# Eight of the twelve groups of layer 1's conditioning move from layer 0's FFN to the recurrence's projections, in halves of 256 columns

## The chip, the cores and the metric

The kernel runs on one core of one Trainium2 chip. The metric is the device time of one execution in microseconds, as the median of three runs. An execution's profile was taken by the hardware profiler; its time is shown beside the runs.

## What is computed

One inference step of a backbone with two layers over 1152 tokens (128 of a context, 1024 of a latent grid), 1024 features wide. Layer 0 mixes tokens by two kinds of attention, layer 1 by a retention and an RWKV-7 recurrence; each layer ends in a SwiGLU FFN. Before each mixer and each FFN the normalised tokens are shifted and scaled, and the results are gated, by six vectors that come from a conditioning vector. There are two of these, one for the context's tokens and one for the latent's. This is the part that the change concerns:

```python
def ada_modulation(cond, w, b):
    m = (jax.nn.silu(cond) @ w + b)[..., None, :]
    return jnp.split(m, 6, axis=-1)
...
    m_ctx = ada_modulation(c_ctx, w_ada[layer], b_ada[layer])
    m_lat = ada_modulation(c, w_ada[layer], b_ada[layer])
    h_ctx = modulate(rms_norm(ctx, norm_mix_g[layer]), m_ctx[0], m_ctx[1])
    h_lat = modulate(rms_norm(lat, norm_mix_g[layer]), m_lat[0], m_lat[1])
```

`w_ada[layer]` is 1024 x 6144 in float32, 25 MB, and it is needed in full for two vectors. The first two of the six vectors of layer 1 are used at the end of layer 0's FFN, where the tokens of layer 1 are normalised; the third after layer 1's mixer; the last three at and after layer 1's FFN.

## The kernel before

**Stages.** In order of time: normalisation and layer 0's projections and attention (to about 956 us of the span), layer 0's FFN (956 to 1797), the recurrence's projections (`rec_proj`, 1797 to 2360), the recurrence itself (`rec_scan`, 2360 to about 2900), its output (`rec_out`), and layer 1's FFN (from 3049). Nearly everything is a matrix product in a split float32 format: each operand is cast by ScalarE into a high part (`wh`, `hH`) and VectorE or GpSimd takes the rest as the low part (`wl`, `hL`); three matmuls make one product (`mm3`, L80 to L84, and L1724 to L1726).

**Who sets the order.** The program is written as generators that hand control back at `yield`. The main one of a stage calls `next(side)` or `background(rate)` between its steps, at a rate that a counter such as `due` sets, so that side work is mixed in. A scheduler of the tile framework then fixes the order of each engine's instructions ahead of time, from a model of the times; on the chip each engine, and each DMA queue, works off its list in that order and waits where something isn't ready.

**The conditioning.** A group is 512 of the 6144 columns, so a layer has twelve. For layer 0 four groups run early on TensorE; its other eight, and all twelve of layer 1, go through `ada_vec` (L165). For each group it takes the eight row blocks k of 128 rows: SyncE loads a tile `aw` of 128 x 512 (L128), and VectorE multiplies it by the conditioning value of each partition, once for each of the two vectors, into the accumulator `aacc` (L179 for the first block, L181 for the others). After the eighth block TensorE sums over the partitions with a column of ones (L189: eight small matmuls in the code, sixteen in the trace), and VectorE adds the bias (`ada_mod`, L149, L153). The load of a block is issued right after the instructions on the block before it. A group is nine steps (`yield`s).

**Where layer 1's twelve groups ran.** All in layer 0's FFN. `ffn` (L1615) first makes the two first tiles of 128 hidden columns plainly, then the others (f = 2 to 21) as seven products of blocks each (L1724 to L1726, operands `hH`, `T1`, `T2`, `T3`; results `A`, `B`, `D`, `E` in PSUM). From the fifteenth product on it calls `next(side)` at a rate of 0.44 (L1755). Then `ffn_out` (L1844) does the output projection in six groups of hidden tiles and calls it at 0.48 (L1898). In the first part `self.ap` is the FFN's own pool (L2079), which gives the tag `aw` no number of buffers, and so one; in the second part `aw` is another name for `raw` (L1802), of which layer 0 has five and layer 1 six (L2074). `raw` holds the FFN's weights before the split.

**The recurrence's projections.** `rec_proj` goes through 15 blocks of 256 columns of `w_in_rec` (`proj_cols`, L788 on). For a block, eight weight tiles `wraw` of 128 x 256 are loaded by SyncE (L793, four buffers), cast to `wh` by ScalarE (L74) and their low part made by VectorE (L75); `wh` and `wl` have nine buffers each, so one tile of the next block fits beside the eight of the present one. Then come 9 tiles of tokens (L817 to L819) or 6 tiles of features (L82 to L84), in four PSUM banks `mm`. Each tile ends in a `sink`: ScalarE copies it into `fst` (two buffers) and SyncE stores it (L834, L844). `background(rate)` is called twice per tile: it advances the preparation of the RWKV operands (`prep`, on ScalarE, VectorE and GpSimd) and the retention (`ret`).

## Time and profile before

| | us |
|---|---|
| median of three runs | 3854.85 |
| lowest and highest run | 3852.91, 3861.53 |
| the profiled execution | 3851.15 |
| its span | 3849.4 |

Times inside the profile count from the start of the span. A row of a view by stage gives the stretch, its length, and for each engine the busy time and, as x, the number of instructions, then the granted TensorE clock as a share of full speed, the share of time in which the DMA engines were busy, and GB/s. Engines are PE (TensorE), PEld (its weight loads), DVE (VectorE), ACT (ScalarE), POOL (GpSimd) and SPq (SyncE's instruction queue, which issues DMAs). A row of a group or a timeline names line, engine, operation, result <- operands, shape and number; what stands in brackets or behind a bar is the idle time ahead of it and what ended it. A waiting row reads: who <- for whom: us in total, times, the longest.

### The profile page before, as it was taken

What the parts mean: (1) busy time and instruction counts of PE and PEld (TensorE: products, weight loads), DVE (VectorE), ACT (ScalarE), POOL (GpSimd) and SP (SyncE); (2) the same over time, 40 slices, a digit from 0 to 9 for tenths busy, and PEclk for the clock granted to TensorE, in tenths of its full rate; (3) what the DMA queues carried; (4) which work ended last, traced back from release to release, by engine and by line L of the source; (5) the groups of instructions that cost most, each with busy time, mean ns of one, the idle gap of its engine ahead of it and who ended that gap; (6) DMA issues with size and microseconds to landing.
All of it is one profiled execution on the core that took longest, in us unless ns stands there. A gap on an engine that the chain in (4) does not pass through costs nothing.

```text
span 3849.4 us, 67037 instructions
## 1 busy us (share of the span) xinstructions
PE 3661.5 (95%) x24885; PEld 3444.4 (89%) x24885; DVE 2272.7 (59%) x5106; ACT 1404.6 (36%) x3361; POOL 1100.4 (29%) x1450
## 2 busy tenths in 40 slices
PE   7999997999999999999999998999998999999998
PEld 4899996999899999999989886877777899999998
DVE  6677864665945556665244556766665774444434
ACT  3445444555333333225332333233322533334221
POOL 2000002112222224333011323665662322324430
PEclk9999997999999999999999998999999999999999
DMA  6433325542223334442334336232223212223321
GB/s 209 125 94 107 113 69 133 133 109 61 64 85 108 91 99 143 149 137 86 106 105 130 115 129 212 58 88 65 65 60 108 62 60 75 75 73 107 116 88 61
DMA packets 425399, 392.16 MB, mean 102 GB/s; under 512 B 68172, under 2 KB 370376, under 8 KB 423536
## 3 DMA queue, kind: packets, MB, share of 16 engines
q1 hardware_dynamic: 406640, 376.29, 32.3%
q10 hardware_dynamic: 13152, 7.27, 0.7%
q0 software_dynamic: 5280, 4.31, 0.6%
q8 instruction: 197, 3.23, 0.3%
q14 instruction: 130, 1.06, 0.1%
HBM read 289.32 MB, written 98.33 MB: 101 GB/s over the span
## 4 chain that ended last, share of the span: by engine, by line
PE 74%; DVE 8%; DMA 8%; POOL 3%; issue 2%; ACT 2%; SPq 0%; DVEq 0%; ACTq 0%; POOLq 0%
PE mm L82 8%; PE mm L84 8%; PE mm L83 8%; PE A L1726 3%; PE A L1724 3%; PE A L1725 3%; PE o L482 3%; DMA aw<-in_w_ada_dram 2%; PE E L1724 2%; PE E L1725 2%; PE mm L350 2%; PE E L1726 2%; PE mm L352 2%; PE mm L351 2%; DVE aacc L181 2%
## 5 line engine op out<-in xcount | busy, mean ns | idle before, releaser
L729 DVE SCALAR_TENSOR_TENSOR x<-mm,mod,x 128x128 f32<-128x128 f32 (+1 forms) x576 | 277.2, 512 | 238.7 <-PE mm L84 237.9
L1636 POOL TENSOR_TENSOR wl<-raw,wh 128x512 fp32r<-128x512 f32 x120 | 167.1, 1392 | 567.2 <-ACT wh L1635 541.3
L1635 ACT CAST wh<-raw 128x512 fp32r<-128x512 f32 x288 | 178.3, 620 | 306.4 <-PE A L1725 107.4
L181 DVE SCALAR_TENSOR_TENSOR aacc<-aw,v,aacc 128x512 f32<-128x512 f32 x280 | 228.7, 849 | 75.2 <-DMA aw<-in_w_ada_dram 74.7
L350 PE MATMUL mm<-wh,hH 128*128 128x384 f32 x576 | 200.8, 349 | 11.5 <-ACT wh L74 4.7
L352 PE MATMUL mm<-wh,hL 128*128 128x384 f32 x576 | 195.8, 341 | 4.6 <-DVE hL L261 4.6
L351 PE MATMUL mm<-wl,hH 128*128 128x384 f32 x576 | 197.3, 342 | 1.0 <-DVE wl L75 0.9
L82 PE MATMUL mm<-hH,wh 128*128 128x384 f32 x528 | 184.6, 351 | 2.6 <-ACT wh L74 2.6
L84 PE MATMUL mm<-hH,wl 128*128 128x384 f32 x528 | 180.3, 344 | 3.4 <-DVE rst L867 2.1
L83 PE MATMUL mm<-hL,wh 128*128 128x384 f32 x528 | 180.3, 342 | 0.0
L1636 DVE TENSOR_TENSOR wl<-raw,wh 128x512 fp32r<-128x512 f32 x168 | 118.8, 708 | 102.1 <-ACT wh L1635 98.3
L397 POOL TENSOR_TENSOR rm<-rm,rm 128x128 f32<-128x128 f32 (+1 forms) x40 | 27.0, 676 | 461.2 <-DVE rm L387 329.0
L75 DVE TENSOR_TENSOR wl<-wraw,wh 128x256 fp32r<-128x256 f32 (+1 forms) x184 | 90.1, 508 | 108.3 <-ACT wh L74 78.7
L1150 PE MATMUL A<-AR,BK 64*128 64x256 f32 x576 | 116.8, 418 | 31.3 <-DVE KK L1154 18.6
L524 ACT ACTIVATE P<-S,mx 128x384 f32<-128x384 f32 (+1 forms) x200 | 112.2, 570 | 88.8 <-DVE mx L522 86.6
L82 PE MATMUL mm<-mh,owh 128*128 128x384 f32 x384 | 138.5, 375 | 5.2 <-ACT owh L74 2.7
L83 PE MATMUL mm<-ml,owh 128*128 128x384 f32 x384 | 132.5, 345 | 0.0
L84 PE MATMUL mm<-mh,owl 128*128 128x384 f32 x384 | 131.3, 342 | 1.2 <-DVE owl L75 1.2
L350 PEld LDWEIGHTS mm<-wh,hH 128*128 128x128 f32 x576 | 110.2, 191 | 16.2 <-ACT ist L368 7.7
L817 PE MATMUL mm<-wh,hH 128*128 128x256 f32 x432 | 124.0, 290 | 0.0
L1150 PEld LDWEIGHTS A<-AR,BK 64*128 64x128 f32 x576 | 75.4, 194 | 53.1 <-issue 20.0
L818 PE MATMUL mm<-wl,hH 128*128 128x256 f32 x432 | 122.4, 285 | 0.0
(540 smaller groups left out, 12501.5 us busy)
## 6 DMA issues: line engine op xcount, KB each, us to landing
raw<-in_w_ffn_in_dram SPq DMA_DIRECT2D x176, 256.0 KB
aw<-in_w_ada_dram SPq DMA_DIRECT2D x160, 256.0 KB
raw<-hdr SPq DMA_DIRECT2D x132, 192.0 KB
hdr<-c SPq DMA_DIRECT2D x160, 144.0 KB
raw<-in_w_ffn_out_dram SPq DMA_DIRECT2D x88, 256.0 KB
F<-stg SPq DMA_DIRECT2D x34, 640.0 KB
stg<-st SPq DMA_DIRECT2D x12, 1536.0 KB
qkv<-ist SPq DMA_DIRECT2D x72, 192.0 KB
```

Of the source, the lines that this page charges most:

```text
L82: mm(out, lhsT=wh, rhs=xh, start=first, stop=False)
L83: mm(out, lhsT=wh, rhs=xl, start=False, stop=False)
L84: mm(out, lhsT=wl, rhs=xh, start=False, stop=last)
L181: nc.vector.scalar_tensor_tensor(acc[:, c, :], w[:, 0, :], s, acc[:, c, :], op0=ALU.mult, op1=ALU.add)
L350: mm(pt[:, :ncol], lhsT=hH[k][:, c], rhs=WH[k], start=k == 0, stop=False)
L351: mm(pt[:, :ncol], lhsT=hH[k][:, c], rhs=WL[k], start=False, stop=False)
L352: mm(pt[:, :ncol], lhsT=hL[k][:, c], rhs=WH[k], start=False, stop=k == KT - 1)
L729: self.nc.vector.scalar_tensor_tensor(x[f][:, c], pt[:, a:b], self.mod[l][jg][:, f, cd : cd + 1], x[f][:, c], op0=ALU.mult, op1=ALU.add)
L1636: eng.tensor_tensor(wl, w, wh, op=ALU.subtract)
L1724: mm(o, lhsT=wh[:, ks], rhs=xh, start=new and k == 0, stop=False, skip_group_check=True)
L1725: mm(o, lhsT=wh[:, ks], rhs=xl, start=False, stop=False, skip_group_check=True)
L1726: mm(o, lhsT=wl[:, ks], rhs=xh, start=False, stop=k == 3, skip_group_check=True)
```

## The change

Layer 0's FFN keeps groups 0 to 3 of layer 1, in its output projection alone, where they still use the buffers of `raw`; the calls in the products go, and with them the FFN's own `aw` and `aacc` buffers in that part. `raw` gets six buffers in both layers. Groups 4 to 11 go to `rec_proj`: `background` calls their generator at a rate of 0.72 for each of the 216 times it is called, whatever else it does. `ada_vec` gets the pool and a width: with 256 it goes through a group in two halves, each with its own eight loads (128 x 256, 128 KB), its own accumulation, four of L189's eight matmuls and its own additions. The pool of `rec_proj` names no number of buffers for `aw`, so there is one, and one of `aacc`. The matmuls' results take one of the four PSUM banks `mm`.

The core of the diff:

```diff
-    def ada_load(self, l, cg, k, n, pool):
-        w = self.t(pool, [P, n, 512], tag="aw")
+    def ada_load(self, l, cg, k, n, pool, c0=0, w=512):
+        t = self.t(pool, [P, n, w], tag="aw")
...
-        self.nc.sync.dma_start(w, src[:, k : k + n, cg * 512 : (cg + 1) * 512])
-        return w
+        self.nc.sync.dma_start(t, src[:, k : k + n, cg * 512 + c0 : cg * 512 + c0 + w])
+        return t
...
-    def ada_vec(self, l, cgs):
+    def ada_vec(self, l, cgs, pool, wd=512):
...
-        w, acc, p2 = self.ada_load(l, cgs[0], 0, 1, self.ap), None, None
-        for n, cg in enumerate(cgs):
+        seq = [(cg, c0) for cg in cgs for c0 in range(0, 512, wd)]
+        w, acc, p2 = self.ada_load(l, cgs[0], 0, 1, pool, 0, wd), None, None
+        for n, (cg, c0) in enumerate(seq):
             for k in range(KT):
                 if k == 0:
                     if p2 is not None:
-                        self.ada_mod(l, cgs[n - 1], p2)
-                    acc = self.t(self.ap, [P, 2, 512], tag="aacc", bufs=1)
+                        self.ada_mod(l, *was, wd)
+                    acc = self.t(pool, [P, 2, wd], tag="aacc", bufs=1)
...
             p2 = self.t(self.nps, [P, 512], tag="mm")
-            for f in range(4):
+            was = cg, p2, c0
+            for f in range(wd // P):
...
+            side, owed = self.ada_vec(1, range(4, 12), p, 256), 0.0
...
             def background(rate):
 
-                nonlocal due
+                nonlocal due, owed
+                owed += 0.72
+                while owed >= 1:
+                    owed -= 1
+                    next(side, None)
...
             while preps:
                 background(1.0)
+            fin(side)
...
-        C, store, due = {}, [], 0.0
-        self.nps = _Alias(ps.pool, {"mm": "D"})
+        C, store = {}, []
...
-            if n >= 14:
-                due += 0.44
-                while due >= 1:
-                    due -= 1
-                    next(side, None)
...
-        self.nps, self.ap = ps, _Alias(p, {"aw": "raw"})
...
-            p = _Bufs(es.enter_context(self.pool(f"ff{l}", "right" if l else "left")), {"raw": 6 if l else 5, "wh": 3, "wl": 3, "c": 4})
+            p = _Bufs(es.enter_context(self.pool(f"ff{l}", "right" if l else "left")), {"raw": 6, "wh": 3, "wl": 3, "c": 4})
...
-            side = iter(()) if l else self.ada_vec(1, range(12))
+            side = iter(()) if l else self.ada_vec(1, range(4), _Alias(p, {"aw": "raw"}))
```

How the order of the instructions changes, at the places of which the prediction speaks. Line numbers in the new order are those of the changed file, one to nine higher than before; x2 is one instruction for each of the two vectors.

VectorE in the middle of layer 0's products, at about 1217 to 1229 us of the profile before (`c` and `raw` are the FFN's tiles, `wl` its weight splits):

```order
L1798 TENSOR_TENSOR c_13651<-c_13583,c_13651 128x288
L1772 TENSOR_TENSOR c_13774<-c_13774,B_13794 128x288
L181 SCALAR_TENSOR_TENSOR aacc_13789<-aw_13938,v_5_67,aacc_13789 128x512 x2
L1772 TENSOR_TENSOR c_13775<-c_13775,B_13807 128x288
L1636 TENSOR_TENSOR wl_13825<-raw_13662,wh_13824 128x512
L181 SCALAR_TENSOR_TENSOR aacc_13789<-aw_14055,v_5_67,aacc_13789 128x512 x2
L181 SCALAR_TENSOR_TENSOR aacc_13789<-aw_14125,v_5_67,aacc_13789 128x512 x2
L1636 TENSOR_TENSOR wl_13891<-raw_13660,wh_13890 128x512
L1786 TENSOR_TENSOR c_13920<-c_13918,E_13864 128x288
```

and at a like place after the change:

```order
L1801 TENSOR_TENSOR c_13823<-c_13759,c_13823 128x288
L1799 TENSOR_TENSOR c_13760<-c_13760,E_13780 128x288
L1645 TENSOR_TENSOR wl_13908<-raw_13699,wh_13907 128x512
L1801 TENSOR_TENSOR c_13824<-c_13760,c_13824 128x288
L1775 TENSOR_TENSOR c_13938<-c_13938,B_13952 128x288
L1775 TENSOR_TENSOR c_13939<-c_13939,B_13965 128x288
L1645 TENSOR_TENSOR wl_13983<-raw_13835,wh_13982 128x512
L1707 TENSOR_TENSOR raw_14086<-raw_13950,raw_14086 128x512
L1645 TENSOR_TENSOR wl_14045<-raw_13833,wh_14044 128x512
L1789 TENSOR_TENSOR c_14074<-c_14072,E_14018 128x288
```

The instructions on `aacc` are gone from the products; the rest stands as before.

VectorE in the projections where the run of splits of the fourth block begins (the last splits of the third block ahead of it, at about 1880 us; `kd` belongs to the retention), before:

```order
L75 TENSOR_TENSOR wl_20532<-wraw_20529,wh_20531 128x256
L75 TENSOR_TENSOR wl_20538<-wraw_20535,wh_20537 128x256
L75 TENSOR_TENSOR wl_20796<-wraw_20793,wh_20795 128x256
L1454 TENSOR_SCALAR kd_21236<-rk_21084,KD_20031 128x9x64 x2
L75 TENSOR_TENSOR wl_20802<-wraw_20799,wh_20801 128x256
L75 TENSOR_TENSOR wl_20808<-wraw_20805,wh_20807 128x256
L75 TENSOR_TENSOR wl_20814<-wraw_20811,wh_20813 128x256
L75 TENSOR_TENSOR wl_20820<-wraw_20817,wh_20819 128x256
```

and after the change:

```order
L182 SCALAR_TENSOR_TENSOR aacc_20439<-aw_20442,v_5_67,aacc_20439 128x256 x2
L182 SCALAR_TENSOR_TENSOR aacc_20439<-aw_20474,v_5_67,aacc_20439 128x256 x2
L182 SCALAR_TENSOR_TENSOR aacc_20439<-aw_20493,v_5_67,aacc_20439 128x256 x2
L75 TENSOR_TENSOR wl_20604<-wraw_20601,wh_20603 128x256
L182 SCALAR_TENSOR_TENSOR aacc_20439<-aw_20525,v_5_67,aacc_20439 128x256 x2
L75 TENSOR_TENSOR wl_20610<-wraw_20607,wh_20609 128x256
L75 TENSOR_TENSOR wl_20616<-wraw_20613,wh_20615 128x256
L75 TENSOR_TENSOR wl_20622<-wraw_20619,wh_20621 128x256
L75 TENSOR_TENSOR wl_20628<-wraw_20625,wh_20627 128x256
L182 SCALAR_TENSOR_TENSOR aacc_20439<-aw_20542,v_5_67,aacc_20439 128x256 x2
L75 TENSOR_TENSOR wl_20634<-wraw_20631,wh_20633 128x256
```

Pairs of instructions on `aacc`, each with a load of its own, now stand ahead of the run and inside it.

SyncE at the same place: the stores of the third block's results (`rvd`) and the loads of weights (`wraw`), before:

```order
L834 DMA rvd<-fst_20734 128x256
L834 DMA rvd<-fst_20762 128x256
L793 DMA wraw_20823<-in_w_in_rec_dram 128x256
L793 DMA wraw_20829<-in_w_in_rec_dram 128x256
L793 DMA wraw_20835<-in_w_in_rec_dram 128x256
L793 DMA wraw_21009<-in_w_in_rec_dram 128x256
L834 DMA rvd<-fst_20790 128x256
L793 DMA wraw_21015<-in_w_in_rec_dram 128x256
```

and after the change:

```order
L837 DMA rvd<-fst_20488 128x256
L128 DMA aw_20493<-in_w_ada_dram 128x256
L837 DMA rvd<-fst_20520 128x256
L128 DMA aw_20525<-in_w_ada_dram 128x256
L837 DMA rvd<-fst_20556 128x256
L796 DMA wraw_20625<-in_w_in_rec_dram 128x256
L128 DMA aw_20542<-in_w_ada_dram 128x256
L796 DMA wraw_20631<-in_w_in_rec_dram 128x256
L796 DMA wraw_20637<-in_w_in_rec_dram 128x256
L837 DMA rvd<-fst_20588 128x256
```

Loads of `aw` now stand between the stores and among the loads of weights. Over the stage there are 128 of them, in the first 14 of the 15 blocks; between one run of splits and the next stand 8 to 11.

## The prediction

> **What bounds the kernel now.** The page comes first: its span and TensorE's share.

> ```profile
> span 3849.4 us, 67037 instructions
> PE 3661.5 (95%) x24885; PEld 3444.4 (89%) x24885; DVE 2272.7 (59%) x5106; ACT 1404.6 (36%) x3361; POOL 1100.4 (29%) x1450
> ```

> TensorE is busy for 95% of the span, so a microsecond is won only where TensorE waits, or where it does work that could go. The profiled execution took 3851.15 us, of which 1.75 us lie around the span; the median of the runs is 3854.85, 3.7 us above it. I work against the execution and add the 3.7 at the end.

> Next the busy time by stage. Both layers run the same FFN code, but only layer 0's carries the conditioning, so the two FFNs are a controlled pair. The rows are, in order: layer 0's FFN before its products of blocks (L1724 to L1726), their first three column tiles, the other seventeen, and the output projection; then the recurrence's projections; then the four FFN stretches again for layer 1.

> ```profile
> core 0: us, PE busy (x) PEld busy (x) DVE busy (x) ACT busy (x) POOL busy (x), PEclk, DMA share, GB/s
> 956.20:1016.40 60.20, 56.37 (x303) 54.60 (x303) 55.20 (x113) 25.83 (x52) 17.37 (x11) 0.94 0.26 76
> 1016.40:1094.00 77.60, 71.32 (x505) 70.24 (x506) 54.70 (x106) 29.31 (x65) 23.36 (x17) 0.96 0.23 68
> 1094.00:1505.60 411.60, 396.49 (x2953) 394.17 (x2953) 232.36 (x397) 139.61 (x298) 119.63 (x92) 0.99 0.34 100
> 1505.60:1795.10 289.50, 289.50 (x1712) 289.12 (x1710) 189.40 (x345) 78.17 (x155) 110.65 (x101) 1.00 0.42 133
> 1797.00:2360.00 563.00, 548.84 (x3745) 494.75 (x3747) 269.30 (x758) 183.06 (x428) 107.19 (x106) 0.99 0.38 121
> 3048.90:3103.10 54.20, 53.95 (x303) 53.59 (x304) 46.58 (x110) 28.73 (x61) 12.53 (x13) 0.97 0.18 55
> 3103.10:3176.30 73.20, 70.47 (x507) 69.45 (x506) 46.39 (x94) 27.86 (x61) 26.14 (x17) 0.95 0.23 70
> 3176.30:3554.90 378.60, 378.60 (x2857) 378.60 (x2857) 166.22 (x305) 144.77 (x300) 118.98 (x92) 1.00 0.27 80
> ```

> The same two stretches of layer 0, for the conditioning's own matmuls (L189) alone:

> ```profile
> 1094.00:1505.60 411.60, 11.03 (x96) 11.28 (x96) 0.99 0.34 100
> 1505.60:1795.10 289.50, 11.03 (x96) 11.55 (x96) 1.00 0.42 133
> ```

> 2953 matmuls less these 96 are 2857, exactly layer 1's number, yet layer 0 takes 411.6 us against 378.6. The waits of TensorE and then of VectorE in that stretch say why:

> ```profile
> PE A L1726 <- DVE wl L1636: 10.4, 5, 2.3
> PE E L1724 <- DVE c L1786: 4.6, 3, 1.8
> ```

> ```profile
> DVE aacc L181 <- DMA aw<-in_w_ada_dram: 51.7, 29, 2.9
> ```

> One such case in order of time, on SyncE's queue, VectorE and TensorE:

> ```profile
> 1223.80 0.33 SPq L128 DMA_DIRECT2D aw<-in_w_ada_dram  x1
> 1228.02 0.33 SPq L128 DMA_DIRECT2D aw<-in_w_ada_dram  x1
> ```

> ```profile
> 1226.58 1.41 DVE L181 SCALAR_TENSOR_TENSOR aacc<-aw,v,aacc 128x512 f32<-128x512 f32 x2 [2.81 <-DMA aw<-in_w_ada_dram]
> 1227.91 0.68 DVE L1636 TENSOR_TENSOR wl<-raw,wh 128x512 fp32r<-128x512 f32 x1
> ...
> 1230.79 2.26 DVE L181 SCALAR_TENSOR_TENSOR aacc<-aw,v,aacc 128x512 f32<-128x512 f32 x2 [1.83 <-DMA aw<-in_w_ada_dram]
> ...
> 1233.58 0.68 DVE L1636 TENSOR_TENSOR wl<-raw,wh 128x512 fp32r<-128x512 f32 x1
> ```

> ```profile
> 1234.31 0.61 PE L1726 MATMUL A<-hH,wl 128*128 128x288 f32 x1 [2.29 <-DVE wl L1636]
> ```

> The pool has one buffer for `aw`. VectorE waits for the load (1223.80 to 1226.58: 2.78 us), uses it in two instructions (1.41), and only then the next load goes out at 1228.02: a round of 4.2 us. The weight splits `wl` stand behind such pairs, and TensorE in the end behind a split: the one of 1233.58 held it for 2.29 us.

> **The change part by part.**

> *Layer 0's FFN, products.* All `aacc` rows (the accumulator's) have left the products, as the order in the section on the change shows at the place quoted above; the four groups that stay come in the output projection. What is left is layer 1's program, in which TensorE waits for nothing (378.6 busy of 378.6), so I see nothing that would be late next, and the seventeen tiles should take layer 1's time: 378.6 - 411.6 = **-33.0** (15.1 of it idle TensorE, 11.0 its L189, 6.9 matmuls drawn out after stalls). The 60.2 + 77.6 us ahead of them are 10.4 above layer 1's 54.2 + 73.2. VectorE does a first group there, by the row of the `aacc` instructions alone,

> ```profile
> 956.00:1016.40 60.40, 0.00 (x0) 0.00 (x0) 13.22 (x16) 0.94 0.26 77
> ```

> and `raw` has five buffers against layer 1's six; the change cures both, but part of the rest may be layer 0's own start. Between 0 and -10.4 I take **-6**.

> *Output projection.* Six groups' L189 took 11.03 us there; four remain: two groups at 1.84 are **-3.7**. TensorE has no idle time in this stretch, so nothing else is to be had.

> *Recurrence's projections, TensorE.* The eight groups' matmuls are as many in halves as whole: 128 of the recorded instructions at 11.03/96 = 0.115, **+14.7**. TensorE is busy 548.8 of 563 us here, so all of it counts.

> *The same, VectorE, loads and stalls.* For the times:

> ```profile
> L181 DVE SCALAR_TENSOR_TENSOR aacc<-aw,v,aacc x280: 726/745/1850, 38.5 to 1713.0; 128x512 f32<-128x512 f32 x140
> ```

> ```profile
> L729 DVE SCALAR_TENSOR_TENSOR x<-mm,mod,x 128x256 f32<-128x256 f32 x144 | 68.3, 474 | 0.0
> ```

> ```profile
> 1904.61 0.81 SPq L793 DMA_DIRECT2D wraw<-in_w_in_rec_dram  x2
> ```

> ```profile
> 1906.70 0.41 ACT L74 CAST wh<-wraw 128x256 fp32r<-128x256 f32 x1 [1.07 <-DMA wraw<-in_w_in_rec_dram]
> ```

> ```profile
> DVE mod L149 <- PE mm L189: 4.1, 4, 1.1
> ```

> A half instruction costs 0.474, not half of 0.745: 256 of them are about 115 us (a few are the cheaper first ones). They fit by volume: 269 of 563 us become 384. A load of 128 KB, the new size, took 2.09 us to its first use (1904.61 to 1906.70). There is again one buffer, so a round is 2.1 + 0.9 + 0.1 to wake SyncE = 3.1 us, and each of 16 halves adds about 1.0 for the turn of the accumulator. 128 rounds are 413 us in the 505 that the weight loads span:

> ```profile
> L793 SPq DMA_DIRECT2D wraw<-in_w_in_rec_dram x150: 327/382/1634, 1797.0 to 2302.3; - x150
> ```

> The rows above give the price of halving: the round falls from 4.2 to 3.1, not to 2.1. [...]

> On average the rounds fit; locally they don't. The runs of weight splits mark the blocks of 256 columns (VectorE, then TensorE's use of the sixth split of the middle run):

> ```profile
> 1854.48 1.50 DVE L75 TENSOR_TENSOR wl<-wraw,wh 128x256 fp32r<-128x256 f32 x4 [12.50 <-ACT wh L74]
> 1880.12 1.49 DVE L75 TENSOR_TENSOR wl<-wraw,wh 128x256 fp32r<-128x256 f32 x4 [12.39 <-ACT wh L74]
> 1883.10 0.43 DVE L75 TENSOR_TENSOR wl<-wraw,wh 128x256 fp32r<-128x256 f32 x1 [1.49 <-ACT wh L74]
> 1904.15 1.94 DVE L75 TENSOR_TENSOR wl<-wraw,wh 128x256 fp32r<-128x256 f32 x4 [18.91 <-PE mm L83]
> ```

> ```profile
> 1883.20 0.51 PE L84 MATMUL mm<-hH,wl 128*128 128x384 f32 x2
> 1884.96 0.34 PE L84 MATMUL mm<-hH,wl 128*128 128x384 f32 x1
> ```

> Around 1880.12, VectorE did nothing but splits, and SyncE's queue held only result stores and weight loads. In the new order, shown in the section on the change, pairs of `aacc` instructions stand inside the run of splits, and `aw` loads between the stores and the weight loads. An `aw` load waits for VectorE to free the buffer, and the stores and weight loads behind it wait too. The order holds 11 rounds between the runs of 1854.48 and 1880.12, 25.6 us plus 0.9 of new matmuls: 11 x 3.1 + 1.0 = 35.1, late by 8.6. The next 24.0 + 0.9 us hold nine, 28.9: late by 4.0. Of these 12.6 us about 4 are in hand (the second split, done by 1880.5, is used at 1883.20, the sixth, done at 1883.53, at 1884.96): 8. In the other blocks the rounds fit: 108 x 3.1 + 14 = 349 us in the 505.3 - 49.6 = 455.7 that are left. What stalls there is the run of splits: by the order 17 pairs stand inside runs, each holding the rest back by up to 2.6 us against 1.4 to 2.7 in hand; half a microsecond each on average makes 9. So **+17**. The lower end is 5: 12.6 less the 2.7 and less the 4.8 from 1880.12 to 1884.96. The upper is 36: 17 pairs at 2.1, the mean of the five waits on `wl` above (10.4/5), nearest in kind but with less in hand. A gain is excluded, since nothing is taken away in this stage.

> Its end stays as it is: the last pair stands ahead of the last block's splits, whose loads end at 2302.3, and the stage ends at 2360. Costed at nothing: 128 issues on SyncE at 0.33 (42 us of its 563), 16.8 MB more (121 becomes 151 GB/s, against 133 in the output projection today, where TensorE does not wait), and a PSUM bank of the four that the projections turn through, held for one step of the chain. If that cover fails, the case is B below.

> Sum: -33.0 - 6 - 3.7 + 14.7 + 17 = **-11.0** us: 3851.15 becomes 3840.2, and the median of runs 3843.9.

> **The rivals.** *A, the stalls hide:* 5 instead of 17, net -23.0, 3832. For it: VectorE is idle over half the stage. Against: 51.7 us of waits for only 43 loads in the FFN, by the row

> ```profile
> aw<-in_w_ada_dram SPq DMA_DIRECT2D x43, 256.0 KB
> ```

> *B, the chain of loads becomes the bound,* the slower side. Rounds fill the 505.3 us plus the 42.7 gained from (505.3 + 42.7 - 16)/128 = 4.16 us on. Large transfers pass on the same queue:

> ```profile
> stg<-st SPq DMA_DIRECT2D x12, 1536.0 KB
> ```

> At 4.4 us a round the chain is 579, 74 over, in place of 14.7 + 17: +31 net, 3886. For it: the FFN's measured 4.2. Against: that is with double loads and instructions. [...]

> *C, the boundaries eat the gain:* 28 of stalls, net 0, 3855. For it: SyncE held up at the very time when the last three weights of a block are asked for. That the change does not relieve the FFN is not a rival: no `aacc` row is left in the products.

> **How the numbers follow.** About 0.2%, 7.7 us, is what a measurement can tell from no change. Forecast 0.43 (stalls 10 to 24, net -18 to -4), A 0.19, C 0.22 (-4 to +8), B 0.16. Faster: A and three quarters of the forecast, 0.51. Same: the other quarter and 0.18 of C, 0.29. Slower: 0.20. Range: lowest -33 - 10 - 3.7 + 14.7 + 5 = -27; highest -33 + 0 - 3.7 + 14.7 + 36 = +14; with 1 us on each side 3827 to 3870. It leaves out most of B.

> **What would show it.** Layer 0's products at 379 us for seventeen tiles, with no wait for `aw`; L189 in the projections at about 15 us; the rounds at 3.1; TensorE's waits for `wl` at the block boundaries. I am wrong if the projections grow by over 45 us, or if layer 0's seventeen tiles stay above 390.

## The result, and the profile after

The changed kernel takes 3920.8 us (median of four runs, 3918.1 to 3928.5) against 3855.2 before on the same chip: a ratio of 1.0171, 95% interval 1.0151 to 1.019. It is slower by 66 us, where 11 us faster were forecast, and outside the range. Its profiled execution, the slowest of the four, took 3928.5 us; the rows below are of it, so they have to explain 77 us against the profile before, some 12 more than the medians differ by. The page of the changed kernel:

```profile
span 3926.7 us, 67300 instructions
PE 3709.8 (94%) x24885; PEld 3487.6 (89%) x24885; DVE 2273.1 (58%) x5244; ACT 1408.3 (36%) x3361; POOL 1096.2 (28%) x1450
PEclk9999998999999999998999996988888999999999
```

and the row of the clock in 40 slices before:

```profile
PEclk9999997999999999999999998999999999999999
```

TensorE does the same 24885 recorded instructions and is busy 48 us longer. In slices 25 and 27 to 31, where the recurrence runs, the granted clock has fallen. The stages are cut at four marks that both kernels have: the first matmul on `T3h` in layer 0's FFN, the first use of a weight's low part in the projections, the same in their last block, and the first matmul on `T3h` in layer 1's FFN. A row gives the stretch, its length, and per engine busy time and instructions; the last three numbers are clock, DMA share and GB/s. Before:

```profile
956.20:1801.00 844.80, 814.96 (x5471) 808.63 (x5471) 537.43 (x976) 276.18 (x576) 272.60 (x219) 0.98 0.36 108
1801.00:2306.20 505.20, 504.03 (x3391) 454.68 (x3392) 232.70 (x657) 167.14 (x390) 88.65 (x82) 1.00 0.37 116
2306.20:3048.90 742.70, 675.37 (x5078) 569.08 (x5077) 483.03 (x1115) 231.56 (x540) 382.09 (x799) 0.94 0.30 90
3048.90:3849.40 800.50, 785.68 (x5319) 783.90 (x5319) 385.12 (x758) 269.20 (x566) 244.92 (x199) 0.99 0.27 82
```

and after:

```profile
960.00:1760.70 800.70, 789.35 (x5344) 786.62 (x5344) 435.50 (x838) 280.34 (x576) 267.69 (x219) 0.99 0.30 93
1760.70:2325.90 565.20, 527.20 (x3482) 476.76 (x3483) 337.78 (x926) 162.16 (x383) 87.33 (x80) 0.97 0.42 130
2325.90:3126.60 800.70, 729.37 (x5116) 615.30 (x5114) 479.86 (x1122) 237.41 (x547) 385.08 (x801) 0.88 0.29 86
3126.60:3926.70 800.10, 783.93 (x5319) 782.27 (x5319) 386.28 (x758) 268.33 (x566) 243.75 (x199) 0.99 0.27 82
```

So layer 0's FFN gained 44.1 us; the projections lost 60.0; the third stretch (the end of the projections, the recurrence and its output, "the scan" from here on) lost 58.0; 3.8 us are lost ahead of the FFN, where nothing was changed, and 0.4 gained behind: 3.8 - 44.1 + 60.0 + 58.0 - 0.4 = 77.3, the difference of the two spans. The recurrence got no new instruction; of the moved work only the last 8 of the 128 small matmuls, about 1 us, lie in the third stretch.

The same rows show what kind of time was lost. In the scan TensorE's busy time rose from 675.37 to 729.37 us, by 54.0, for the same work, and its idle time (length less busy) only from 67.3 to 71.3. In the projections it is the other way: idle time rose from 1.2 to 38.0 us, busy time by 23.2, most of which is the moved matmuls.

**The FFN.** The seventeen tiles of the products after the change:

```profile
1088.60:1467.40 378.80, 378.80 (x2859) 378.80 (x2858) 167.34 (x305) 144.00 (x298) 118.73 (x91) 1.00 0.26 80
```

They take layer 1's 378.6 us to within 0.2, as forecast, and TensorE has no idle time.

**The projections.** What VectorE's instructions on `aw` waited for there (times in us, number of times, the longest), and the matmuls that read the sums:

```profile
DVE aacc L182 <- DMA aw<-in_w_ada_dram: 137.3, 83, 4.8
DVE mod L149 <- PE mm L192: 25.6, 9, 7.8
```

```profile
L192 PE MATMUL mm<-ones,aacc 128*128 128x1 f32 x120 | 16.6, 248 | 18.2 <-DVE aacc L182 18.2
```

TensorE stood 18.2 us ahead of these matmuls. One such end of a half, first on VectorE, then on TensorE:

```profile
1818.67 0.87 DVE L182 SCALAR_TENSOR_TENSOR aacc<-aw,v,aacc 128x256 f32<-128x256 f32 x2
1821.79 0.88 DVE L182 SCALAR_TENSOR_TENSOR aacc<-aw,v,aacc 128x256 f32<-128x256 f32 x2 [2.25 <-DMA aw<-in_w_ada_dram]
1824.98 0.88 DVE L182 SCALAR_TENSOR_TENSOR aacc<-aw,v,aacc 128x256 f32<-128x256 f32 x2 [2.30 <-DMA aw<-in_w_ada_dram]
1828.07 0.88 DVE L182 SCALAR_TENSOR_TENSOR aacc<-aw,v,aacc 128x256 f32<-128x256 f32 x2 [2.21 <-DMA aw<-in_w_ada_dram]
1831.21 0.88 DVE L182 SCALAR_TENSOR_TENSOR aacc<-aw,v,aacc 128x256 f32<-128x256 f32 x2 [2.26 <-DMA aw<-in_w_ada_dram]
```

```profile
1831.84 0.56 PE L192 MATMUL mm<-ones,aacc 128*128 128x1 f32 x2 [7.78 <-DVE aacc L182]
```

Five rounds stand one behind the other in VectorE's list, with nothing between them. Each takes 3.1 us, the forecast length, of which VectorE stands 2.2; everything that is queued behind, and TensorE in the end, waits. Of TensorE's 38 us of idle time in this stage about 35 were ended by VectorE. For weights that came late it hardly waited, neither for the high parts (first row) nor for the splits (the other two), so it was not the weight loads behind the `aw` loads in SyncE's queue that held it:

```profile
PE mm L82 <- ACT wh L74: 0.2, 1, 0.2
PE mm L84 <- DVE wl L75: 2.7, 3, 1.3
PE mm L821 <- DVE wl L75: 1.4, 1, 1.4
```

By the records of the clock TensorE was granted half its clock for 10.2 us from 1826.4, that is 2.3 us after the wait of 7.78 us began, and again for 13.7 us from 1857.2, inside the wait at the next such end. Over the projections it ran 35 us at half clock, before 3.

**The scan.** The same records give 85 us at half clock before and 195 after: half of the difference, 55 us, is about the 54.0 by which TensorE's busy time grew. Its idle time is hardly larger: the wait that holds it longest there, for VectorE's copies `KK`, is 17.1 us between 2400 and 2920 us before, and 18.8 in the same length from 2420 us after. But it waits otherwise. Before and after:

```profile
PE A L1150 <- DVE KK L1154: 17.1, 15, 1.5
```

```profile
PE A L1159 <- DVE KK L1163: 18.8, 9, 3.6
```

Fewer waits, and longer ones. One of these places on TensorE, before:

```profile
2540.93 1.14 PE L1150 MATMUL A<-AR,BK 64*128 64x256 f32 x8
2542.50 0.66 PE L1224 MATMUL I<-ident,MM 128*128 128x128 f32 x4 [0.43 <-DVE MM L1244]
2542.99 1.06 PE L1235 MATMUL I<-E,TC 128*128 128x128 f32 x8
2545.51 2.15 PE L1150 MATMUL A<-AR,BK 64*128 64x256 f32 x8 [1.46 <-DVE KK L1154]
```

and after:

```profile
2707.76 1.16 PE L1159 MATMUL A<-AR,BK 64*128 64x256 f32 x8
2708.84 1.16 PE L1249 MATMUL I<-X,WT 128*128 128x128 f32 x8
2713.43 1.82 PE L1159 MATMUL A<-AR,BK 64*128 64x256 f32 x5 [3.42 <-DVE KK L1163]
```

The matmuls `A` of a step come in four sets, and matmuls `I` of another step stand between the sets. Ahead of the last set the trace has 12 of them before and 8 after, and 3.42 us of idle time in one piece instead of 0.43 and 1.46. The copies `KK` come late because VectorE's own list has the copy `BT` ahead of them, and that waits for GpSimd, 0.72 us before and 2.05 after the change:

```profile
2543.16 1.33 DVE L1203 COPY BT<-MB 32x256 f32<-32x256 f32 x1 [0.72 <-POOL MB L1201]
```

```profile
2711.28 1.33 DVE L1212 COPY BT<-MB 32x256 f32<-32x256 f32 x1 [2.05 <-POOL MB L1210]
```

The clock follows at once, in stretches of 3.41 us after the change:

```profile
2707.04:2710.45 3.41, 2.96 (x24) 1.00 0.14 53
2710.45:2713.87 3.42, 0.44 (x2) 1.00 0.00 0
2713.87:2717.28 3.41, 3.41 (x12) 0.50 0.13 19
2717.28:2720.69 3.41, 3.41 (x19) 0.50 0.12 19
2720.69:2724.11 3.42, 3.42 (x22) 0.50 0.10 10
```

The order in which the scheduler put TensorE's instructions at this place of a step, before and after:

```
L1150 MATMUL A_27889<-AR_5513_27745,BK_5514_27750 128x256 x2
L1150 MATMUL A_27890<-AR_5513_27745,BK_5514_27750 128x256 x2
L1224 MATMUL I_27654<-ident_60,MM_27310 128x128 x4
L1235 MATMUL I_27660<-E_27518,TC_4986_25679 128x128 x4
L1150 MATMUL A_27901<-AR_5522_27770,BK_5523_27775 128x256 x2
```

```
L1159 MATMUL A_28171<-AR_5593_28027,BK_5594_28032 128x256 x2
L1159 MATMUL A_28172<-AR_5593_28027,BK_5594_28032 128x256 x2
L1249 MATMUL I_27949<-X_27947,WT_27935 128x128 x4
L1159 MATMUL A_28183<-AR_5602_28052,BK_5603_28057 128x256 x2
```

The program text of the scan was not touched, and its instructions are the same; the scheduler's model arrived at another order of them, by up to 66 places on TensorE. It repeats from step to step.

### The profile page after: what moved, and what is told of

Read it like the earlier page. It is cut to its first block, busy times and chain, and to the rows that moved or that the text cites. A ratio compares the mean times of both kernels' runs of the same rounds, so it can differ in the third digit from the quotient of the medians.

```text
span 3926.7 us, 67300 instructions
## 1 busy us (share of the span) xinstructions
PE 3709.8 (94%) x24885; PEld 3487.6 (89%) x24885; DVE 2273.1 (58%) x5244; ACT 1408.3 (36%) x3361; POOL 1096.2 (28%) x1450
## 3 DMA queue, kind: packets, MB, share of 16 engines
q14 instruction: 131, 1.07, 0.1%
## 4 chain that ended last, share of the span: by engine, by line
PE 67%; DMA 12%; DVE 10%; POOL 3%; issue 3%; ACT 2%; SPq 0%; DVEq 0%; ACTq 0%; POOLq 0%
PE mm L82 7%; PE mm L84 6%; PE mm L83 6%; DMA aw<-in_w_ada_dram 4%; PE A L1733 3%; PE A L1734 3%; PE A L1735 3%; PE o L485 3%; DVE aacc L182 3%; PE E L1734 2%; PE E L1733 2%; PE E L1735 2%; PE mm L353 2%; PE mm L355 2%; PE mm L354 2%
## 5 line engine op out<-in xcount | busy, mean ns | idle before, releaser
L182 DVE SCALAR_TENSOR_TENSOR aacc<-aw,v,aacc 128x256 f32<-128x256 f32 (+1 forms) x392 | 242.6, 656 | 146.5 <-DMA aw<-in_w_ada_dram 145.9
L84 PE MATMUL mm<-hH,wl 128*128 128x384 f32 x528 | 181.1, 346 | 5.0 <-DVE wl L75 2.7
L83 PE MATMUL mm<-hL,wh 128*128 128x384 f32 x528 | 181.3, 344 | 0.0
L1159 PE MATMUL A<-AR,BK 64*128 64x256 f32 x576 | 133.4, 448 | 31.8 <-DVE KK L1163 19.7
L1707 DVE TENSOR_TENSOR raw<-raw,raw 128x512 f32<-128x512 f32 x40 | 27.7, 692 | 193.9 <-POOL raw L1706 193.9
L1159 PEld LDWEIGHTS A<-AR,BK 64*128 64x128 f32 x576 | 85.5, 209 | 55.8 <-issue 24.4
L83 PE MATMUL mm<-ml,owh 128*128 128x384 f32 x384 | 133.8, 348 | 0.0
L84 PE MATMUL mm<-mh,owl 128*128 128x384 f32 x384 | 131.8, 343 | 0.9 <-DVE owl L75 0.9
## 6 DMA issues: line engine op xcount, KB each, us to landing
raw<-in_w_ffn_in_dram SPq DMA_DIRECT2D x176, 256.0 KB
aw<-in_w_ada_dram SPq DMA_DIRECT2D x96, 256.0 KB
raw<-in_w_ffn_out_dram SPq DMA_DIRECT2D x88, 256.0 KB
stg<-st SPq DMA_DIRECT2D x12, 1536.0 KB
```

The lines of the kernel that those rows point to most:

```text
L83: mm(out, lhsT=wh, rhs=xl, start=False, stop=False)
L84: mm(out, lhsT=wl, rhs=xh, start=False, stop=last)
L182: nc.vector.scalar_tensor_tensor(acc[:, c, :], w[:, 0, :], s, acc[:, c, :], op0=ALU.mult, op1=ALU.add)
L1159: mm(pts[h][:, j * 256 : j * 256 + 256], lhsT=BK[hs, j, :], rhs=AR[hs], start=True, stop=True)
```

## The experiments

Two things had to be explained: the 58 us of the scan (order, or something that the moved work leaves behind), and the growth of the projections beyond 31.7 us. The table has what the twelve kernels gave; lengths and the us at half clock are of one profiled execution each, between the marks used above, and the waits are VectorE's idle time in the projections until an `aw` load. The profiled executions of e4, e6, e7, e10 and e11 took 13, 17, 10, 4 and 16 us less than their kernel's median, so their lengths lie rather low.

| kernel | median us | ratio to before, 95% | projections | half clock there | waits for `aw` | scan | half clock there |
|---|---|---|---|---|---|---|---|
| before | 3855.2 | | 505.2 | 3 | 0 | 742.7 | 85 |
| after | 3920.8 | 1.0151 to 1.019 | 565.2 | 35 | 141 | 800.7 | 195 |
| e1 | 3870.5 | 1.0032 to 1.0073 | 572.2 | 55 | 144 | 741.3 | 75 |
| e2 | 3893.5 | 1.009 to 1.0123 | 505.0 | 3 | 0 | 779.6 | 157 |
| e3 | 3803.4 | 0.9858 to 0.9891 | 508.3 | 7 | 0 | 739.6 | 89 |
| e4 | 3910.4 | 1.012 to 1.0194 | 593.8 | 68 | 116 | 743.2 | 58 |
| e5 | 3872.7 | 1.0049 to 1.0099 | 574.9 | 41 | 163 | 738.7 | 79 |
| e6 | 3837.7 | 0.9952 to 0.9993 | 532.8 | 14 | 47 | 732.4 | 51 |
| e7 | 3838.5 | 0.995 to 0.9981 | 534.0 | 21 | 43 | 734.9 | 55 |
| e8 | 3864.5 | 1.0026 to 1.0065 | 553.3 | 24 | 105 | 749.3 | 106 |
| e9 | 3828.9 | 0.9932 to 0.9968 | 534.7 | 23 | 0 | 736.4 | 65 |
| e10 | 3831.3 | 0.9944 to 0.9987 | 531.0 | 14 | 18 | 734.0 | 75 |
| e11 | 3849.3 | 0.9961 to 1.0009 | 532.2 | 12 | 46 | 738.2 | 75 |
| e12 | 3875.5 | 1.0055 to 1.0087 | 569.3 | 42 | 141 | 744.7 | 82 |

The kernel before took 3849.7, 3851.8 and 3849.0 us beside the three sets of four (e1 to e4, e5 to e8, e9 to e12), each of which ran on a chip of its own.

**e1 and e2: the scan's order exchanged.** The edit notes the instructions that `rec_scan` traces and chains those of each engine in a given order (`SCAN_ORDER`, read from the other kernel's schedule); the chain says only which comes first (`NoSync`).

```diff
+    def pin(self, i0):
+        dep = lambda: mybir.DependencyInfo(mybir.DependencyClass.NoSync, mybir.DependencyReason.DATA)
+        ins = [i for i in list(self.nc.cur_bb.bb.instructions)[i0:] if type(i).__name__ != "BassTilePoolBoundary"]
+        for e, moves in json.loads(zlib.decompress(base64.b85decode(SCAN_ORDER))).items():
+            own = [i for i in ins if str(i.engine) == "EngineType." + e]
+            own = [own[n + m] for n, m in enumerate(moves)]
+            for a, b in zip(own, own[1:]):
+                self.tc.add_manual_dep(b, a.name, dep(), reason="pin")
...
+            i0 = len(self.nc.cur_bb.bb.instructions)
             self.rec_scan(hp)
+            self.pin(i0)
```

> The changed kernel, with the instructions of rec_scan held on every engine in the order that they had before. Theory 1 (the order): the scan lost its time because its instructions were put in another order, which gathers TensorE's idle time and lowers the granted clock; then about 3866 us (3855 to 3880), with 85 to 110 us of the scan at half clock instead of 195. Rival (what the moved work leaves behind: buffers, transfers, a later start): 3921 us, give or take 5, half clock as in the changed kernel.

> The kernel before, with the instructions of rec_scan held in the order that they have in the changed kernel, and nothing else. Theory 1 (the order): slower by the 55 us that the scan lost, 3895 to 3915 us, with about 170 to 200 us of the scan at half clock. Rival (what the moved work leaves behind): 3855 us, as before.

Both came out by the order. The changed kernel with the old order in the scan (e1; its projections and its scan):

```profile
1752.60:2324.80 572.20, 536.44 (x3483) 485.27 (x3484) 338.30 (x927) 162.68 (x384) 88.61 (x81) 0.95 0.41 129
2324.80:3066.10 741.30, 675.56 (x5115) 568.40 (x5113) 484.68 (x1122) 234.65 (x547) 382.89 (x801) 0.95 0.31 93
```

and the kernel before with the new order (e2; the scan):

```profile
2311.40:3091.00 779.60, 706.65 (x5078) 597.61 (x5077) 482.00 (x1115) 233.17 (x541) 382.47 (x799) 0.90 0.29 86
```

With the old order the scan takes 741.3 us behind the moved work as well, at a clock of 0.95. With the new one it takes 779.6 in a kernel in which nothing else was changed, 36.9 more than before, and the 157 us at half clock against 85 make 36 of them. The whole kernel e2 is 44 us slower than before on its chip, a little less than was expected. So the order is the cause: with the old one nothing is left for what the moved work leaves behind. The new order alone brings 36.9 of the 58 us. The other 21 appear only together with the moved work, or are the spread between executions; no run parts these.

**e12: TensorE's order alone.** As e1, but only TensorE's list is given.

> As e1, but in the scan only TensorE's instructions are held in the order of before; the other engines' are ordered by the scheduler around that. If TensorE's own queue is what spreads or gathers its idle time: e1's time, 3862 to 3882 us. If the order on VectorE and GpSimd decides: nearer to the changed kernel's 3921 us, above 3895.

The scan (e12):

```profile
2324.30:3069.00 744.70, 677.72 (x5116) 568.57 (x5114) 481.33 (x1122) 234.97 (x547) 383.76 (x801) 0.94 0.31 93
```

Giving TensorE's list is enough: 3875.5 us, as e1 within 5. The scheduler, left free on the other engines, put their instructions nearly in the order of before as well, so the run does not show that TensorE's list alone, with the others' lists as in the changed kernel, would do.

**e3: without the moved groups.**

```diff
-            side, owed = self.ada_vec(1, range(4, 12), p, 256), 0.0
+            side, owed = iter(()), 0.0
+            for j in range(2, 6):
+                nc.vector.memset(self.mod[1][j], 0.5)
```

> As e1, and groups 4 to 11 of layer 1's conditioning are left out altogether (their vectors are set to 0.5). If the growth of the projections is the moved work's own, they are back at 505 us and what is left is the gain of layer 0's FFN: 3812 us (3805 to 3822). If the projections grew for their order or for the emptier FFN ahead of them, they stay at 540 to 565 us, and the time is 3850 to 3870 us.

3803.4 us, 46 less than before, and the projections are back at 508.3 (e3):

```profile
1756.10:2264.40 508.30, 506.04 (x3391) 455.81 (x3392) 232.29 (x656) 166.97 (x390) 88.94 (x82) 0.99 0.36 115
```

The FFN's gain is real and holds to the end, and the growth of the projections is the moved work's own: 572.2 - 508.3 = 63.9 us in e1.

**e4: start after the four blocks that lost most.**

```diff
-            side, owed = self.ada_vec(1, range(4, 12), p, 256), 0.0
+            side, owed, now = self.ada_vec(1, range(4, 12), p, 256), 0.0, 0.0
...
-                owed += 0.72
+                owed += now
...
             fin(first, rk(0), rv(0), rg(0))
+            now = 0.92
```

> As e1, and the moved groups start only after the first four blocks of the projections, at a rate of 0.92 instead of 0.72. If it is the place that costs (44 of the 60 us were lost in these four blocks: TensorE stands 14 us at two ends of halves, and runs 31 us at half clock), then e1's time less about 30 us: 3835 us (3825 to 3845). If it is the work itself, wherever it stands, e1's time within 8 us, with the growth moved to the later blocks.

Neither: 3910.4 us, 40 worse than e1. The first four blocks lost little now (118.7 us against 158.7), but the ten behind them took 475.1 instead of 413.5, at half clock for 58 us. TensorE's waits at the ends of halves went with the work:

```profile
PE mm L198 <- DVE aacc L188: 18.9, 7, 5.5
```

So the first four blocks are not a worse place than the others. Whether the higher rate is what made it worse was not tried by itself. The rate in the code hardly sets where a round stands, either: the first half was computed at 1760 to 1786, long before the first call, since the scheduler puts forward what its model finds ready.

**e5: the sums read two rounds later.** The matmuls of a half move behind the second round of the next one:

```diff
+        lag = (2, 5) if wd < 512 else (0, 0)
...
+                if wd < 512 and n and k == lag[0]:
+                    was = end(*done)
+                if k == lag[1] and was is not None:
+                    self.ada_mod(l, *was, wd)
...
-                    acc = self.t(pool, [P, 2, wd], tag="aacc", bufs=1)
+                    acc = self.t(pool, [P, 2, wd], tag="aacc", bufs=1 if wd == 512 else 2)
...
-            p = _Bufs(es.enter_context(self.pool("rA")), {"wraw": 4, "wh": 9, "wl": 9, "fst": 2, "kh": 2, "st": 2, "kt": 4, "tmp": 8})
+            p = _Bufs(es.enter_context(self.pool("rA")), {"wraw": 4, "wh": 9, "wl": 9, "fst": 2, "kh": 2, "st": 2, "kt": 4, "tmp": 7})
```

> As e1 (scan in the order of before), and in the projections the matmuls that read a half's sums are written two rounds of the next half later, with two buffers of aacc (and seven instead of eight of tmp, for the room). Theory (TensorE stands at the ends of halves, and the half clock follows from that): the 17 us of waits before these matmuls and most of the 20 us that the half clock costs go, 3835 to 3848 us. Rival (VectorE's standing at each load is what delays all that is queued behind it, wherever the sums are read): 3860 to 3872 us.

The theory of the ends of halves falls: 3872.7 us, nothing gained. The waits at these matmuls are gone, and TensorE waits as long for the weight splits that stand behind the rounds in VectorE's list (e5, its matmuls and their weight loads):

```profile
PE mm L90 <- DVE wl L81: 13.6, 11, 3.1
PEld mm L90 <- DVE wl L81: 18.3, 13, 3.4
```

**e6, e7, e10, e11: more buffers for the loads.** e6 is e1 with

```diff
-            p = _Bufs(es.enter_context(self.pool("rA")), {"wraw": 4, "wh": 9, "wl": 9, "fst": 2, "kh": 2, "st": 2, "kt": 4, "tmp": 8})
+            p = _Bufs(es.enter_context(self.pool("rA")), {"wraw": 4, "wh": 9, "wl": 9, "fst": 2, "kh": 2, "st": 2, "kt": 4, "tmp": 7, "aw": 2})
```

e7 adds e5's edit (`tmp` 6), e10 has `"aw": 3` and `"tmp": 6`, and e11 is e6 with the scan left to the scheduler.

> As e1, and aw has two buffers in the projections (tmp seven), so that a load runs beside the round before it. Theory (ends of halves): a round falls from 3.2 us to below 2.5, but TensorE's matmuls that read the sums are ordered by the same model and some still wait: 3840 to 3860 us. Rival (VectorE's standing at the loads is the whole cause): the waits of VectorE for aw fall from 144 us below 40, and the time to 3825 to 3840 us.

> As e1, with the edits of e5 and e6 together (tmp six). What is left over the kernel without the groups (3803 us) is then the 128 small matmuls on TensorE, some 15 us, and little else: 3815 to 3830 us. If six buffers of tmp are too few, or VectorE's work itself is the cost, 3840 us or more.

> As e6, with three buffers of aw and six of tmp. Theory 2: VectorE's waits for aw fall from 47 us to below 15, the projections from 533 us to about 525, the time to 3826 to 3836 us. If what is left in e6 is not the loads: e6's 3838 us within 5.

> As e6, without holding the scan to its order of before: the scheduler orders it anew. The projections stay at 533 us. Theory 1 says that the time follows the order which comes out, with nothing in the edit to steer it: from 3835 us, where it is like that of before, to 3895 us, where it is like that of the changed kernel, and half the half-clock time that is added to the scan is the time lost there.

What VectorE's `aacc` instructions waited for in e6, and the projections:

```profile
DVE aacc L188 <- DMA aw<-in_w_ada_dram: 47.1, 54, 4.5
```

```profile
1753.80:2286.60 532.80, 522.06 (x3511) 471.91 (x3512) 341.72 (x931) 165.56 (x391) 92.06 (x83) 0.99 0.46 142
```

The projections fall by 39.4 us against e1 (this execution was the fastest of its ten), the kernel's median by 33. e7 gives the same time (projections 534.0 us): with the loads ahead, where the sums are read does not matter. The third buffer (e10) takes the waits to 18 us and the projections only to 531.0. In e11, with nothing to steer the scan, the scheduler's order came out nearer to that of before than to the changed kernel's (738.2 us, 75 at half clock). Its median is 11.6 us above e6's and its interval includes no change; the profile, of its fastest execution, does not show where those 11.6 us lie.

**e8: quarters.** As e7 with a width of 128, a rate of 1.36 and `tmp` 8.

> As e7, but by quarters of 128 columns with tmp left at eight: two buffers of aw and two of aacc take the room that one of each took. Twice as many rounds, each of about 0.7 us on VectorE: 180 us of VectorE instead of 125. If only waits cost, 3820 to 3835 us; if VectorE's busy time in the projections costs, 3840 to 3860 us.

3864.5 us, beyond both expectations. VectorE still waits 105 us for loads although there are two buffers: a round is two instructions of 346 ns instead of 479 (medians of e8 and e7), so that it would hide less of a load, and there are 256 of them; this reason is argued, not shown. The scan, too, ran 106 us at half clock in this profile, though its order was that of e1: with one and the same order (e1, e3 to e10) it had 51 to 106, so luck, or what differs between these kernels ahead of the scan, is worth some 25 us of the time, and the 195 of the changed kernel lie far outside.

**e9: one load for all rounds.**

```diff
-                if nxt:
+                if nxt and wd == 512:
                     w = self.ada_load(l, nxt[0], nxt[1], 1, pool, nxt[2], wd)
```

> As e1, but of the 128 loads of aw in the projections only the first is made, and every round computes from it: the sums are not those of groups 4 to 11, all of VectorE's and TensorE's work for them stays. Theory 2 (VectorE's standing at the loads is the cost): the projections take about 523 us, that is 508 without the groups and 15 for the 128 small matmuls, and the time is 3815 to 3828 us. Rival (VectorE's 125 us of work in front of the splits costs as well): 3835 us or more.

3828.9 us; the projections take 534.7 where 523 were expected:

```profile
1757.50:2292.20 534.70, 527.46 (x3510) 475.10 (x3511) 334.02 (x931) 166.35 (x389) 90.34 (x82) 0.98 0.35 110
```

```profile
L198 PE MATMUL mm<-ones,aacc 128*128 128x1 f32 x120 | 14.3, 238 | 0.0
```

That parts e1's 63.9 us: 572.2 - 534.7 = 37.5 for the loads, with the half clock that follows; 14.3 for the small matmuls; 12.1 that stay without any load. The 37.5 are for VectorE's standing and not for the traffic or SyncE's work: e6 and e10 make all 128 loads, and their projections, 532.8 and 531.0 us, are no longer than these. What the 12.1 are was not settled: VectorE's work ahead of other work (114.5 us in e9), or the scheduler's other order of the stage.

Of the kernels that compute everything, e6, e7 and e10 are faster than the one before on their chips, with ratios of 0.9973, 0.9965 and 0.9966; their intervals all lie below 1 and do not part the three. They hold the scan's order; without that (e11) no gain is shown.

## Why the prediction was wrong

- *Layer 0's FFN, -33.0 - 6 - 3.7 = -42.7.* Right: -44.1 between the marks, and the seventeen tiles at 378.8. The two smaller terms were each off by some, -9.2 ahead of these tiles and -2.1 behind them, and the errors cancel in part, by luck.
- *L189 in the projections, +14.7.* Right: 14.3 for 120 recorded instructions of 128 where nothing delays them.
- *The round, 3.1 us.* Right: 3.1 from one to the next in the rows above.
- *Stalls, +17, at most 36.* Wrong: 60.0 - 14.7 = 45.3. The step that failed is "108 x 3.1 + 14 = 349 us in the 455.7 that are left", that is, rounds that fit outside two crowded blocks and cost only where a pair stands inside a run of splits, half a microsecond each. Rounds that fit on average do not stand at an average distance. The scheduler put those of a half one behind the other, at the pace of its model; on the chip VectorE stood 2.2 us in each, 141 us in all, and whatever was queued behind a chain came late by the sum. Nor did TensorE wait where the prediction looked: for splits `wl` 4.1 us in all, but 18.2 us ahead of the small matmuls at the ends of halves, a wait for which the sum had no term. Two buffers take away 39 us, so the stalls are mostly this. TensorE's idle time grew by 36.8 us; the rest is busy time, 23.2 us more, of which 14.3 are the small matmuls, so that the half clock, for which the sum had no term either, is about 9 of the 45.
- *"Its end stays as it is"*, and a sum with no term for anything behind the projections. Wrong, by 58.0 us, the largest error: the scan was put at nothing without a reason, and the runs show that its new order took the clock from it (195 us at half clock instead of 85). The prediction looks at the new order up to the end of the moved work and not beyond, although the order of the scan stood in the two schedules, and TensorE's clock of 0.94 there before said that this stage did not have its full clock. Without the scan's loss (e1, 3870.5 us) the time would still have lain 27 us above the forecast, just over the top of the range, and 21 us above the kernel before on its chip: the stalls alone turn the sign.
- *The rivals.* B had the sign, and its mechanism, the chain of loads, was the nearest: but no run shows its 4.4 us a round, rounds of 3.1 us did not fill the stage, and the price came from where they stood. C's 28 us of stalls at the boundaries were too few. No rival spoke of the scan.
- The prediction's own mark was reached: "I am wrong if the projections grow by over 45 us". They grew by 60.

## What to carry to other kernels

Work that fits by volume costs by where it stands in an in-order list (the 128 rounds were put at 413 us in 505, and the stage grew by 60.0): a load that its reader waits for on the spot needs a second buffer before it is moved into a stage in which that reader feeds TensorE (it took 39.4 us off the projections here, e6 against e1). Where a scheduler sets the order, read it to the end of the program and not only where the change is, and take the stages that run below full clock first (the scan, at 0.94 before); holding one stage in its old order tells in one run whether order is the cause. And the clock did not go by the sum of TensorE's idle time: in 520 us of the scan 17 us of waits for `KK` in fifteen pieces came with 49 us at half clock, 19 in nine pieces with 130.

## What the runs showed of the hardware

```profile
2654.16:2657.57 3.41, 2.36 (x10) 1.00 0.04 10
2657.57:2660.98 3.41, 3.41 (x19) 0.50 0.21 29
2660.98:2664.40 3.42, 3.42 (x22) 0.50 0.10 10
2664.40:2667.81 3.41, 3.41 (x15) 0.50 0.00 0
2667.81:2671.22 3.41, 3.41 (x37) 1.00 0.02 5
```

The half clock then mostly lasts 10.2 or 13.7 us, although the rows show TensorE busy throughout. What besides idle time decides when the clock falls stays open.
